# Softmax attention keys kept once for each head of a pair, with zeros on the other head's rows

## The chip, the core and the metric

The kernel runs on one core of one Trainium2 chip. The metric is the device time of one execution in microseconds (us), the median of several runs. The core has five engines that run beside one another and meet through semaphores: TensorE (PE, the matrix engine; its weight loads are listed apart as PEld), VectorE (DVE), ScalarE (ACT), GpSimd (POOL) and SyncE (SP, which issues DMAs). A matmul has a stationary operand, which is loaded first (a weight load), and a moving one that streams against it.

## What is computed

One decoder block on 512 tokens of 1024 features, all float32. Cut to what matters here:

```python
h    = rms_norm(x, norm1_g)
proj = h @ w_in                      # 9744 columns, cut into the parts of all branches
A    = dilated_attention(...)        # softmax attention, 3 groups of 8 heads of 64 features
B    = gated_linear_attention(...)
mixed = sigmoid(gA) * (A @ w_attn_branch) + sigmoid(gB) * (B @ w_gla_branch)
x    = x + mixed @ w_out
x    = x + relu(rms_norm(x) @ w_ff_up) ** 2 @ w_ff_down

# inside a group of the softmax attention, a head with E = 64 features
scores = (q @ k.T) * E ** -0.5       # q, k: rms_norm over the 64 features of the head, with gains
scores = where(valid, scores, -inf)
p      = exp(scores - max(scores))
o      = (p @ v) / sum(p)
```

The three groups look back over windows of 128, 512 and 2048 tokens with dilations 1, 4 and 16. Their outputs are merged by the softmax denominators.

## The kernel before

Weights come in as raw float32 tiles by SP's DMA queue (`raw_load`, line 112), are cut on ACT and DVE into two float32r parts that add up to them (`split`), and go through PE three times: high by high, low by high, high by low. `mm_tok` (lines 151 to 153) makes tokens by features, with the normed input as the stationary operand; `mm_cols` (lines 132 to 134) makes features by tokens, with the weights as the stationary operand. These projections fill most of PE's time. Helper `act` (line 74) records every ACT activation, `tt` (line 77) every DVE tensor-by-tensor operation.

The softmax attention has two parts around the change. `qkv(g, ...)` projects one group: queries, keys, values, one after the other through `mm_tok`. For each of four tiles of 128 tokens it evicts the bank (ACT), squares (POOL), reduces and scales (DVE, ACT), and puts off a `turn`: four transposes on PE (line 324) and one eviction on ACT that writes the transposed tile. These turns are issued while the next projection runs, behind a matmul of it. The transposed queries `q1T`, `q2T`, `q3T` and keys `k1T`, `k2T`, `k3T` have the shape [128, 4, 512]: 128 rows are the 64 features of two heads, 4 is the pair of heads, 512 are tokens. The keys are scaled on the way by the column `gqk`.

`attend` makes one tile of 128 queries for all 8 heads. The score of a head is one f32 matmul whose operands are the 64 rows of that head (`r`, rows 0 to 63 or 64 to 127). It is written into a bank of the pool `aux` (three banks). DVE adds the mask and takes the maximum (line 353), ACT the exponential, PE transposes (line 359), DVE copies the transposed tile to SBUF (line 361), PE multiplies with the values (line 365). `scores1` (line 375) serves the first group with 128 or 256 keys, directly behind `qkv(0)`; `scores23` (line 390) serves the other two groups together, 128 keys each, behind `qkv(1)` and `qkv(2)`. The second and third group use the tokens in permuted order (`hT.perm`, every fourth column).

The order on each engine is made by a scheduler from the program: it fills PE between the steps of `attend` with matmuls of the next projections, so scores, transposes, value matmuls and projections alternate on PE. Big tiles live in 16 numbered slots, `slot(i, ...)`, and a slot is written again only when its readers are done. Slots 14 and 15 were empty until the linear attention's `qT` and `kT`, and slot 10 goes from `k1T` to the linear attention's values.

Of the kernel before, what the change touches and what calls it, by code (L numbers as in the profile page):

```python
# [8 lines left out]
F32 = mybir.dt.float32  # L9
# [3 lines left out]
AF = mybir.ActivationFunctionType  # L13
# [3 lines left out]
P = 128  # L17
S = 512
# [4 lines left out]
E = 64  # L23
# [18 lines left out]
def kernel(ctx: ExitStack, tc: tile.TileContext, x, norm1_g, w_in, q_g, k_g,  # L42
                             gate_up, gate_bias, out_g, branch_bias, w_attn, w_gla, w_out,
                             norm2_g, w_up, w_down, out):
    nc = tc.nc
# [12 lines left out]
    def slot(i, shape, name, dt=F32):  # L58
        return slots.tile(shape, dt, name=name, tag=f"s{i}")
# [13 lines left out]
    def act(o, i, f, **kw):  # L73
        nc.scalar.activation(o, i, f, **kw)  # L74
# [8 lines left out]

# [1 line left out]
    ident = consts.tile([P, P], F32, name="ident")  # L85
# [8 lines left out]

# [1 line left out]
    n_split = [0]  # L96
# [18 lines left out]
    def w_cols(w, nk, c0, n):  # L115
        """weights as the stationary operand: yields (hi, lo) of [P, nk, 128], one output block each"""
        step = 2048 // nk
        piece = 1024 // nk
        for c in range(c0, c0 + n, step):
            raw = raw_load(w, 0, nk, c, step)  # L120
            for q in range(0, step, piece):
                hi, lo = split(raw[:, :, q:q + piece], [nk, piece])
                for b in range(0, piece, P):
                    yield hi[:, :, b:b + P], lo[:, :, b:b + P]

    def mm_cols(wp, rhs, nk):
        """[128 features, 512 tokens] = block^T . rhs"""
        b = mm_bank()
        hi, lo = wp
        for k in range(nk):  # L130
            rh, rl = rhs(k)
            nc.tensor.matmul(b, hi[:, k], rh, start=(k == 0), stop=False)  # L132
            nc.tensor.matmul(b, hi[:, k], rl, start=False, stop=False)  # L133
            mm = nc.tensor.matmul(b, lo[:, k], rh, start=False, stop=(k == nk - 1))  # L134
            if turns and k in (3, 7):
                with tc.issue_after(mm.ins):
                    turns.pop(0)()
        return b

    def mm_tok(w, c0, lhs, r0=0, nk=KB):  # L140
        """four banks [128 tokens, 512 features] = lhs^T . w[:, c0:c0+512]"""
        banks = [mm_bank() for _ in range(NT)]
# [16 lines left out]
    class Split:  # L159
        """[128 features, nk blocks, 512 tokens] in two float32r parts"""  # L160

# [15 lines left out]
    def rsqrt(o, ss, n, w):  # L177
        """o = (ss / n + eps) ** -0.5, with a Newton step behind the tables"""
        v = sm(w, "rv")
        nc.vector.tensor_scalar(v, ss, 1.0 / n, EPS, op0=OP.mult, op1=OP.add)  # L180
        y = sm(w, "ry")
        act(y, v, AF.Ln)
        act(y, y, AF.Exp, scale=-0.5)
        nc.vector.scalar_tensor_tensor(v, y, -0.5, v, op0=OP.mult, op1=OP.mult)
        tt(v, v, y, OP.mult)
        nc.vector.scalar_tensor_tensor(o, v, 1.5, y, op0=OP.add, op1=OP.mult)

# [1 line left out]
    hT = Split("hT", (0, 1), (2, 3))  # L189
# [55 lines left out]

# [1 line left out]
    with tc.issue_after(last.ins):  # L247
        qk_cols = consts.tile([P, 2], F32, name="qk_cols")
        for j, g in enumerate((q_g, k_g)):
            for hf in range(2):  # L250
# [3 lines left out]
                                       op0=OP.mult, op1=OP.mult)  # L254
        # attention masks: 0 where the key is visible, a large negative number elsewhere
        mask_a = consts.tile([P, 256], F32, name="mask_a")
# [14 lines left out]

        # gated linear attention: which (s, t) pairs a level of the block tree covers
        def block_mask(name, w, segs):
            """segs: (offset, groups, columns a group, rows a group, first row, rows); 1 where row s is covered"""
            g = consts.tile([P, w], U8, name=name)
# [25 lines left out]

# [1 line left out]
    def qkv(g, lhs, sq, sk, sv):  # L303
        res = []
        for kind, s in ((0, sq), (1, sk)):
            banks = mm_tok(w_in, kind * 1536 + g * 512, lhs)
            dst = slot(s, [P, 4, S], f"a{kind}{g}")
            for i in range(NT):
# [11 lines left out]

                def turn(s2=s2, d=dst[:, :, i * P:(i + 1) * P], kw={"scale": gqk} if kind else {}):
                    b = aux()
                    for k in range(4):
                        nc.tensor.transpose(b[:, k * P:(k + 1) * P], s2[:, k * P:(k + 1) * P], ident)  # L324
                    act(d, b.rearrange("p (k t) -> p k t", k=4), AF.Copy, **kw)

                later.append(turn)
            res.append(dst)
        banks = mm_tok(w_in, 3072 + g * 512, lhs)
# [9 lines left out]
    def attend(o_idx, i, scores, values, width, mask, dst):  # L339
        """one tile of 128 queries, all 8 heads; scores/values give the parts of `width` keys"""  # L340
        ob = aux()
# [26 lines left out]

    q1T, k1T, v1 = qkv(0, hT.nat, 9, 10, 11)
    o1 = slot(12, [P, NT, 512], "o1")  # L370

    def scores1(dst, pr, hf, i):
        r = slice(hf * E, hf * E + E)
        lo = max(i - 1, 0) * P
        nc.tensor.matmul(dst, q1T[r, pr, i * P:(i + 1) * P], k1T[r, pr, lo:(i + 1) * P], start=True, stop=True)  # L375

# [5 lines left out]

    q2T, k2T, v2 = qkv(1, hT.perm, 4, 5, 6)
    q3T, k3T, v3 = qkv(2, hT.perm, 7, 8, 13)
    o23 = slot(9, [P, NT, 512], "o23")

    def scores23(dst, pr, hf, i):
        r = slice(hf * E, hf * E + E)
        for n, (q_, k_) in enumerate(((q2T, k2T), (q3T, k3T))):
            nc.tensor.matmul(dst[:, n * P:(n + 1) * P], q_[r, pr, i * P:(i + 1) * P],  # L390
                             k_[r, pr, i * P:(i + 1) * P], start=True, stop=True)

    for i in range(NT):
        attend(1, i, scores23, lambda n, s, i: (v2, v3)[n][:, i, s * E:(s + 1) * E], 256, mask_b, o23)

# [1 line left out]
    lse = consts.tile([P, 64], F32, name="lse")  # L397
# [39 lines left out]

# [1 line left out]
    qT = slot(14, [P, GH, S], "qT")  # L439
# [12 lines left out]
    v_proj(1)  # L452
    # the low-rank gate, both factors in two parts each, all four products in one pass over 128 rows
    lowrank = slot(7, [P, 2, S], "lowrank", F32R)
# [18 lines left out]

# [1 line left out]
    cc = slot(6, [P, GH, S], "cc")  # L475
# [17 lines left out]
    for h in range(GH):  # L493
# [5 lines left out]
        def scores2(left, M):  # L499
            """[s, t] products of each tile's 128 tokens with its 192 columns of M, two tiles a bank"""  # L500
            for i2 in range(2):
# [5 lines left out]

        # the diagonal, and blocks of one token
        M = wide("M")
# [5 lines left out]
        for pd, bv in scores2(kh, M):  # L515
            tt(pd, bv[:, :, :P], ident[:, None, :].to_broadcast([P, 2, P]), OP.mult)
            nc.vector.copy_predicated(pd.rearrange("p i (b two) -> p i b two", two=2)[:, :, :, 1],
                                      pair_mask[1][:, :128].rearrange("p (i b) -> p i b", i=2), bv[:, :, P:])
        # groups of four blocks of m tokens, every pair of blocks in a group
        for m in (2, 8):  # L520
# [18 lines left out]
            for pd, bv in scores2(K, M):  # L539
                for a, off in enumerate((0, 96, 160)):  # L540
# [3 lines left out]
                        pd.rearrange("p i (g x) -> p i g x", g=G)[:, :, :, (a + 1) * m:], gx(qmv), gx(bv))  # L544
        # pairs of blocks of 32 and of 64 tokens
        pdiag = pp.rearrange("p i t -> p (i t)")
        for m in (32, 64):
# [17 lines left out]
            else:  # L565
                act(blocks(pdiag, m)[:64, :, 1], bg[:64, :256].rearrange("p (b m) -> p b m", m=m), AF.Copy)
        # tiles below the diagonal
        c3 = ch.rearrange("p (i t) -> p i t", t=P)
# [9 lines left out]
        act(gt, end.rearrange("p i o -> p (i o)"), AF.Exp, scale=1.0 / TAU)  # L578
        # the state before each tile: [channels, values]
        b = aux()  # L580
# [29 lines left out]

# [1 line left out]
    def gate(f, wp, o):  # L612
        b = mm_cols(wp, hT.rhs, KB)
        # sigmoid(z) = exp(min(z, 0) - ln(1 + exp(-|z|))), z = b + bias
        with tc.high_priority():
# [15 lines left out]

# [1 line left out]
    rs = [slot(14 + j, [P, 2, D], f"rs{j}") for j in range(2)]  # L633
# [13 lines left out]

# [1 line left out]
    oT = Split("oT", (6, 8), (4, 5))  # L649
# [15 lines left out]

# [1 line left out]
    gb = [slot(10 + j, [P, 4, S], f"gb{j}") for j in range(2)]  # L667
# [4 lines left out]

# [1 line left out]
    mx = Split("mx", (0, 1), (2, 3))  # L674
# [8 lines left out]

    # ---- output projection, residual; the second norm's scale is left for the end, since
    # relu(r * u) ** 2 = r ** 2 * relu(u) ** 2 for r > 0 ----
    x2 = [slot(s, [P, 2, D], f"x2{s}") for s in (12, 9)]
# [26 lines left out]

# [1 line left out]
    for half in range(2):  # L715
# [48 lines left out]
```

## Time and profile before

| | us |
|---|---|
| device time, median of 3 runs | 1067.73 (1067.21 to 1067.97) |
| span of the profiled execution | 1065.5 |
| PE busy | 1044.1 (98%) |
| weight loads (PEld) busy | 879.0 (82%) |
| DVE busy | 518.3 (49%) |
| ACT busy | 433.5 (41%) |
| POOL busy | 74.2 (7%) |

The profiled execution's own time is its span; the runs without a profile are 2.2 us above it in the median. PE's clock was granted in full in all slices of the page. Matmul ends are modelled, since matmuls are pipelined: a busy PE need not be PE at its peak, and the start of one matmul to the start of the next tells more than the busy share. A timeline row merges neighbours of the same kind: its length runs from the first start to the last end, and xN is how many they are.

### The profile page before, as it was taken

Reading aid. Unit: us, or ns where it says so; the run is one execution under the profiler, and the core shown is the slowest. Engines: PE = TensorE matmul, PEld = TensorE weight load, DVE = VectorE, ACT = ScalarE, POOL = GpSimd, SP = SyncE. Lnnn points to the kernel's source line nnn. Section 1 sums busy time; section 2 is a strip of 40 time slices with the busy share of each in tenths; the row PEclk is TensorE's granted clock in tenths of the full one; section 3 lists DMA queues with packets and bytes.
Section 4 is the critical chain, followed back from the end, with each engine's and each line's share of the span. In section 5 each row is a group of like instructions: output and inputs, shape, how many; then the busy total and the mean of one; then the engine's idle time right before and its main releaser. Section 6 shows DMA issues by size and latency. Waiting matters only on the chain.

```text
span 1065.5 us, 12435 instructions
## 1 busy us (share of the span) xinstructions
PE 1044.1 (98%) x4888; PEld 879.0 (82%) x4888; DVE 518.3 (49%) x928; ACT 433.5 (41%) x763; POOL 74.2 (7%) x112
## 2 busy tenths in 40 slices
PE   4999999999999999999999999999999999999998
PEld 3888889999888788788888888888888888888886
DVE  4644454434444623988856645444442324444231
ACT  4434343424434424766556852333442113433110
POOL 9110001001000000010103000000000000000000
PEclk9999999999999999999999999999999999999999
DMA  7222102322200223221122232442232323232221
GB/s 257 80 80 79 40 3 78 109 89 79 79 28 17 89 80 99 80 79 54 66 67 93 79 106 92 139 138 79 93 104 81 117 80 119 79 117 82 96 102 39
DMA packets 64505, 92.36 MB, mean 87 GB/s; under 512 B 3328, under 2 KB 37120, under 8 KB 64448
## 3 DMA queue, kind: packets, MB, share of 16 engines
q1 hardware_dynamic: 61056, 86.02, 24.8%
q10 hardware_dynamic: 2976, 5.28, 1.4%
q8 instruction: 38, 0.62, 0.2%
q0 software_dynamic: 416, 0.28, 0.2%
q14 instruction: 19, 0.16, 0.0%
HBM read 89.44 MB, written 2.13 MB: 86 GB/s over the span
## 4 chain that ended last, share of the span: by engine, by line
PE 93%; DVE 3%; ACT 2%; DMA 1%; issue 0%; SPq 0%
PE mm L151 16%; PE mm L153 16%; PE mm L152 16%; PE mm L132 11%; PE mm L133 11%; PE mm L134 10%; PE aux L365 2%; PE aux L390 2%; PE aux L359 2%; PE aux L375 1%; DMA raw<-in_w_in_dram 1%; PE aux L504 1%; PE aux L324 1%; PE aux L602 1%; PE aux L559 1%; DVE wlo L77 1%
## 5 line engine op out<-in xcount | busy, mean ns | idle before, releaser
L77 DVE TENSOR_TENSOR wlo<-wraw,whi 128x1024 fp32r<-128x1024 f32 x157 | 192.5, 1226 | 292.5 <-ACT whi L74 290.7
L74 ACT ACTIVATE whi<-wraw 128x1024 fp32r<-128x1024 f32 x157 | 166.1, 1058 | 330.8 <-PE mm L153 224.9
L151 PE MATMUL mm<-whi,hTh 128*128 128x512 f32 x416 | 171.5, 412 | 4.4 <-ACT hTh L74 4.4
L153 PE MATMUL mm<-whi,hTl 128*128 128x512 f32 x416 | 167.4, 403 | 0.0
L152 PE MATMUL mm<-wlo,hTh 128*128 128x512 f32 x416 | 166.4, 400 | 0.0
L151 PEld LDWEIGHTS mm<-whi,hTh 128*128 128x128 f32 x416 | 102.3, 246 | 15.2 <-ACT hTh L74 5.5
L152 PEld LDWEIGHTS mm<-wlo,hTh 128*128 128x128 f32 x416 | 102.4, 246 | 9.9 <-issue 1.0
L153 PEld LDWEIGHTS mm<-whi,hTl 128*128 128x128 f32 x416 | 102.0, 245 | 10.3 <-issue 1.0
L134 PE MATMUL mm<-xgh,wlo 128*128 128x512 f32 x256 | 99.7, 389 | 0.0
L132 PE MATMUL mm<-xgh,whi 128*128 128x512 f32 x256 | 99.7, 389 | 0.0
L133 PE MATMUL mm<-xgl,whi 128*128 128x512 f32 x256 | 99.6, 389 | 0.0
L132 PE MATMUL mm<-hTh,whi 128*128 128x512 f32 x192 | 77.6, 404 | 0.0
L134 PE MATMUL mm<-hTh,wlo 128*128 128x512 f32 x192 | 76.4, 398 | 0.0
L133 PE MATMUL mm<-hTl,whi 128*128 128x512 f32 x192 | 76.4, 398 | 0.0
L133 PEld LDWEIGHTS mm<-xgl,whi 128*128 128x128 f32 x256 | 48.1, 188 | 10.0
L134 PEld LDWEIGHTS mm<-xgh,wlo 128*128 128x128 f32 x256 | 48.0, 188 | 9.9
L132 PEld LDWEIGHTS mm<-xgh,whi 128*128 128x128 f32 x256 | 48.1, 188 | 9.9
L74 ACT ACTIVATE p<-p,nmx 128x256 f32<-128x256 f32 (+1 forms) x64 | 31.2, 488 | 59.9 <-DVE nmx L353 59.9
L361 DVE COPY pt<-aux 128x512 f32<-128x512 f32 (+1 forms) x32 | 21.1, 659 | 65.0 <-PE aux L359 64.7
L151 PE MATMUL mm<-whi,f0h 128*128 128x512 f32 x128 | 49.8, 389 | 0.0
L152 PE MATMUL mm<-wlo,f0h 128*128 128x512 f32 x128 | 49.8, 389 | 0.0
L153 PE MATMUL mm<-whi,f0l 128*128 128x512 f32 x128 | 49.8, 389 | 0.0
(223 smaller groups left out, 1688.5 us busy)
## 6 DMA issues: line engine op xcount, KB each, us to landing
wraw<-in_w_in_dram SPq DMA_DIRECT2D x36, 1024.0 KB, 5.1
wraw<-in_w_ff_up_dram SPq DMA_DIRECT2D x16, 1024.0 KB, 5.4
wraw<-in_w_ff_down_dram SPq DMA_DIRECT2D x16, 1024.0 KB, 5.0
wraw<-in_w_gla_branch_dram SPq DMA_DIRECT2D x4, 1024.0 KB, 5.1
wraw<-in_w_out_dram SPq DMA_DIRECT2D x4, 1024.0 KB, 5.2
raw<-in_w_in_dram SPq DMA_DIRECT2D x2, 1024.0 KB, 14.2
wraw<-in_w_attn_branch_dram SPq DMA_DIRECT2D x2, 1024.0 KB, 5.2
xr<-in_x_dram ACTq DMA_DIRECT2D x8, 256.0 KB, 4.4
```

The costliest lines, as they stand in the source:

```text
L74: nc.scalar.activation(o, i, f, **kw)
L77: return nc.vector.tensor_tensor(o, a, b, op)
L132: nc.tensor.matmul(b, hi[:, k], rh, start=(k == 0), stop=False)
L133: nc.tensor.matmul(b, hi[:, k], rl, start=False, stop=False)
L134: mm = nc.tensor.matmul(b, lo[:, k], rh, start=False, stop=(k == nk - 1))
L151: nc.tensor.matmul(banks[i], lh, hi[:, kk], start=(k == 0), stop=False)
L152: nc.tensor.matmul(banks[i], lh, lo[:, kk], start=False, stop=False)
L153: mm = nc.tensor.matmul(banks[i], ll, hi[:, kk], start=False, stop=(k == nk - 1))
L359: nc.tensor.transpose(tb[:, n * P:(n + 1) * P], p2[:, n * P:(n + 1) * P], ident)
L361: nc.vector.tensor_copy(pt[:, :w2], tb[:, :w2])
L365: nc.tensor.matmul(ob[:, s * E:(s + 1) * E], pt[:, (m * nk + n) * P:(m * nk + n + 1) * P], values(n, s, i), start=(n == 0), stop=(n == nk ...
L390: nc.tensor.matmul(dst[:, n * P:(n + 1) * P], q_[r, pr, i * P:(i + 1) * P], k_[r, pr, i * P:(i + 1) * P], start=True, stop=True)
```

## The change

The transposed keys are kept twice. Each copy has 128 rows, and on it the rows of one of the two heads are zero: the eviction in `turn` runs once for each copy and scales by one of the two columns of the new constant `gqk2`, which holds `gqk` on 64 rows and 0 on the others. A score matmul then uses all 128 rows of the queries and of the copy of its head. The products on the other head's rows are zeros, so the sum is the same. The second copies lie in slots 14 (`k1T`), 15 (`k2T`) and 10 (`k3T`).

```diff
+        gqk2 = consts.tile([P, 2], F32, name="gqk2")
+        nc.vector.memset(gqk2, 0.0)
+        for hf in range(2):
+            nc.vector.tensor_copy(gqk2[hf * E:(hf + 1) * E, hf:hf + 1], gqk[hf * E:(hf + 1) * E])
...
     def qkv(g, lhs, sq, sk, sv):
         res = []
-        for kind, s in ((0, sq), (1, sk)):
+        for kind, ss_ in ((0, sq), (1, sk)):
             banks = mm_tok(w_in, kind * 1536 + g * 512, lhs)
-            dst = slot(s, [P, 4, S], f"a{kind}{g}")
+            dst = [slot(s, [P, 4, S], f"a{kind}{g}{n}") for n, s in enumerate(ss_)]
...
-                def turn(s2=s2, d=dst[:, :, i * P:(i + 1) * P], kw={"scale": gqk} if kind else {}):
+                def turn(s2=s2, dst=dst, i=i, kind=kind):
                     b = aux()
                     for k in range(4):
                         nc.tensor.transpose(b[:, k * P:(k + 1) * P], s2[:, k * P:(k + 1) * P], ident)
-                    act(d, b.rearrange("p (k t) -> p k t", k=4), AF.Copy, **kw)
+                    for n, d in enumerate(dst):
+                        act(d[:, :, i * P:(i + 1) * P], b.rearrange("p (k t) -> p k t", k=4), AF.Copy,
+                            **({"scale": gqk2[:, n:n + 1]} if kind else {}))
...
-            res.append(dst)
+            res.append(dst if kind else dst[0])
...
-    q1T, k1T, v1 = qkv(0, hT.nat, 9, 10, 11)
+    q1T, k1T, v1 = qkv(0, hT.nat, (9,), (10, 14), 11)
...
     def scores1(dst, pr, hf, i):
-        r = slice(hf * E, hf * E + E)
         lo = max(i - 1, 0) * P
-        nc.tensor.matmul(dst, q1T[r, pr, i * P:(i + 1) * P], k1T[r, pr, lo:(i + 1) * P], start=True, stop=True)
+        nc.tensor.matmul(dst, q1T[:, pr, i * P:(i + 1) * P], k1T[hf][:, pr, lo:(i + 1) * P], start=True, stop=True)
...
-    q2T, k2T, v2 = qkv(1, hT.perm, 4, 5, 6)
-    q3T, k3T, v3 = qkv(2, hT.perm, 7, 8, 13)
+    q2T, k2T, v2 = qkv(1, hT.perm, (4,), (5, 15), 6)
+    q3T, k3T, v3 = qkv(2, hT.perm, (7,), (8, 10), 13)
...
     def scores23(dst, pr, hf, i):
-        r = slice(hf * E, hf * E + E)
         for n, (q_, k_) in enumerate(((q2T, k2T), (q3T, k3T))):
-            nc.tensor.matmul(dst[:, n * P:(n + 1) * P], q_[r, pr, i * P:(i + 1) * P],
-                             k_[r, pr, i * P:(i + 1) * P], start=True, stop=True)
+            nc.tensor.matmul(dst[:, n * P:(n + 1) * P], q_[:, pr, i * P:(i + 1) * P],
+                             k_[hf][:, pr, i * P:(i + 1) * P], start=True, stop=True)
```

No matmul is added, and the order of PE's, POOL's and SP's instructions stays as it was. On PE at the first scores of the first attention, with `a10` for `k1T` and `a00` for `q1T`, there stood before:

```order
L152 MATMUL mm_697<-wlo_805,hTh1_84 128x512
L153 MATMUL mm_697<-whi_804,hTl1_86 128x512
L375 MATMUL aux_845<-a10_629,a00_420 128x128
L375 MATMUL aux_846<-a10_629,a00_420 128x128
L375 MATMUL aux_845<-a10_629,a00_420 128x128
L375 MATMUL aux_846<-a10_629,a00_420 128x128
L151 MATMUL mm_1140<-whi_1146,hTh0_83 128x512
L152 MATMUL mm_1140<-wlo_1147,hTh0_83 128x512
```

and now, with `a100` and `a101` for the two copies of the keys:

```order
L152 MATMUL mm_702<-wlo_813,hTh1_84 128x512
L153 MATMUL mm_702<-whi_812,hTl1_86 128x512
L383 MATMUL aux_854<-a100_633,a000_424 128x128
L383 MATMUL aux_855<-a101_634,a000_424 128x128
L383 MATMUL aux_854<-a100_633,a000_424 128x128
L383 MATMUL aux_855<-a101_634,a000_424 128x128
L151 MATMUL mm_1149<-whi_1155,hTh0_83 128x512
L152 MATMUL mm_1149<-wlo_1156,hTh0_83 128x512
```

The same matmuls stand in the same places; the two heads now read two tiles instead of two halves of one. On ACT, while the values of the first group are projected, there stood before:

```order
L74 ACTIVATE ry_655<-rv_653 128x8
L74 ACTIVATE ry_655<-ry_655 128x8
L74 ACTIVATE whi_1146<-wraw_1144 128x1024
L74 ACTIVATE whi_1174<-wraw_1144 128x1024
L74 ACTIVATE a10_629<-aux_756,gqk_233 128x4x128
```

and now:

```order
L74 ACTIVATE ry_660<-rv_658 128x8
L74 ACTIVATE ry_660<-ry_660 128x8
L74 ACTIVATE whi_1155<-wraw_1153 128x1024
L74 ACTIVATE whi_1183<-wraw_1153 128x1024
L74 ACTIVATE a100_633<-aux_761,gqk2_235 128x4x128
L74 ACTIVATE a101_634<-aux_761,gqk2_235 128x4x128
L74 ACTIVATE ry_676<-rv_674 128x8
```

A second eviction of the same bank stands right behind each of the twelve evictions of keys; nothing else on ACT has changed places.

## Rows read from the trace of the kernel before

**Rows 1.** The page: span, and the chain that ended last by engine.
```profile
span 1065.5 us, 12435 instructions
PE 93%; DVE 3%; ACT 2%; DMA 1%; issue 0%; SPq 0%
```

**Rows 2.** Busy time in two stretches, 92.31:157.40 and 278.57:344.30 us, summed.
```profile
sum 130.82, PE 130.79 PEld 106.72 DVE 56.53 ACT 52.99 POOL 2.69; mean PE 65.39 PEld 53.36 DVE 28.27 ACT 26.49 POOL 1.35
```

**Rows 3.** PE's timeline, second attention: start us, length us, line, out<-in, shapes, count.
```profile
285.43 0.38 PE L359 MATMUL aux<-ident,p 128*128 128x128 f32 x2
285.74 0.48 PE L390 MATMUL aux<-a,a 64*128 64x128 f32 x2
286.15 0.44 PE L359 MATMUL aux<-ident,p 128*128 128x128 f32 x2
286.52 0.93 PE L390 MATMUL aux<-a,a 64*128 64x128 f32 x6
287.38 0.50 PE L133 MATMUL mm<-hTl,whi 128*128 128x512 f32 x1
287.72 1.00 PE L365 MATMUL aux<-v,pt 128*128 128x64 f32 x8
```

**Rows 4.** PE's timeline, first attention, 256 keys wide.
```profile
112.88 0.44 PE L359 MATMUL aux<-ident,p 128*128 128x128 f32 x2
113.25 0.70 PE L375 MATMUL aux<-a,a 64*128 64x256 f32 x2
113.87 0.62 PE L153 MATMUL mm<-whi,hTl 128*128 128x512 f32 x1
114.33 0.40 PE L151 MATMUL mm<-whi,hTh 128*128 128x512 f32 x1
```

**Rows 5.** PE's timeline around the block of sixteen score records.
```profile
278.25 0.40 PE L153 MATMUL mm<-whi,hTl 128*128 128x512 f32 x1
278.57 1.26 PE L390 MATMUL aux<-a,a 64*128 64x128 f32 x16
279.76 0.50 PE L132 MATMUL mm<-hTh,whi 128*128 128x512 f32 x1
280.10 0.40 PE L133 MATMUL mm<-hTl,whi 128*128 128x512 f32 x1
280.33 0.40 PE L134 MATMUL mm<-hTh,wlo 128*128 128x512 f32 x1
```

**Rows 6.** PE's timeline: the first block of scores, what follows, the last block.
```profile
92.31 0.72 PE L375 MATMUL aux<-a,a 64*128 64x128 f32 x8
92.96 0.62 PE L151 MATMUL mm<-whi,hTh 128*128 128x512 f32 x1
...
337.53 1.16 PE L390 MATMUL aux<-a,a 64*128 64x128 f32 x8
```

**Rows 7.** PE's timeline in the linear attention: f32 matmuls over 128 rows.
```profile
468.59 0.59 PE L602 MATMUL aux<-vg,pps 128*128 128x256 f32 x2
469.02 0.59 PE L604 MATMUL aux<-st,q 128*128 128x256 f32 x2
```

**Rows 8.** Lines 359 and 375: durations in ns, least/median/most, first and last start.
```profile
L359 PE MATMUL aux<-ident,p x120: 270/272/332, 94.4 to 342.3; 128*128 128x128 f32 x120
L375 PE MATMUL aux<-a,a x64: 272/376/480, 92.3 to 150.8; 64*128 64x256 f32 x48, 64*128 64x128 f32 x16
```

**Rows 9.** Weight loads' timeline: one of contiguous columns, two of every fourth column.
```profile
287.38 0.19 PEld L133 LDWEIGHTS mm<-hTl,whi 128*128 128x128 f32 x1
...
113.87 0.31 PEld L153 LDWEIGHTS mm<-whi,hTl 128*128 128x128 f32 x1 [0.33 <-issue]
114.08 0.33 PEld L151 LDWEIGHTS mm<-whi,hTh 128*128 128x128 f32 x1
```

**Rows 10.** DVE's timeline: the copy that the value matmuls at 287.72 read.
```profile
286.63 0.69 DVE L361 COPY pt<-aux 128x512 f32<-128x512 f32 x1 [2.27 <-PE aux L359]
```

**Rows 11.** ACT's timeline ahead of the first attention's exponentials.
```profile
89.65 0.69 ACT L74 ACTIVATE a<-aux,gqk 128x512 f32<-128x512 f32 x1 [1.21 <-PE aux L324]
90.35 2.67 ACT L74 ACTIVATE v<-mm 128x512 f32<-128x512 f32 x4
92.91 1.05 ACT L74 ACTIVATE whi<-wraw 128x1024 fp32r<-128x1024 f32 x1
93.86 0.39 ACT L74 ACTIVATE p<-p,nmx 128x128 f32<-128x128 f32 x1
```

## The prediction

> **What bounds the kernel now.** Read the page first: the span is 1065.5 us and TensorE (PE) has 93% of the chain that ended last [rows 1]. A change on another engine therefore counts only where PE comes to wait for it. Then cut out the two stretches in which the softmax scores are computed, 92.31 to 157.40 us and 278.57 to 344.30 us: PE is busy for 130.79 of 130.82 us, VectorE (DVE) for 56.53 and ScalarE (ACT) for 52.99 [rows 2]. But "busy" does not mean that the time is well used. The ends of matmuls are modelled, so what counts is the distance from one start to the next. Look at how the starts stand around the score matmuls (line 375 for the first attention, line 390 for the second). Each f32 product of the program is two records, so there are 64 and 128. They stand on PE in 43 unbroken blocks, the first at 92.31 us and the last at 337.53 us [rows 6].
>
> A run of n records is as long as its starts lie apart plus one duration, 0.27 us for transposes and for 128-wide scores, 0.38 us for 256-wide ones [rows 8]. Two undisturbed transposes take 0.38 us, so their starts are 0.38 - 0.27 = 0.11 us apart. In the block of six scores at 286.52 us the reader sees four losses [rows 3]:
> - **Entry.** The second transpose before it starts at 286.15 + 0.44 - 0.27 = 286.32; the first score follows 0.20 us later, not 0.11: 0.09 lost.
> - **Second record.** The two scores at 285.74 last 0.48 in all, so the second starts 0.48 - 0.27 = 0.21 behind the first. In the six, the other four starts are (0.93 - 0.27 - 0.21) / 4 = 0.112 apart: 0.10 lost.
> - **Exit.** The last score starts at 286.52 + 0.93 - 0.27 = 287.18, the projection behind it at 287.38, 0.20 later: 0.09 lost.
> - **Behind the exit.** That projection needs 0.34 us to the next start, where the undisturbed distance is 280.33 - 280.10 = 0.23 [rows 5]: 0.11 lost. Where transposes come next, their second start is 0.44 - 0.27 = 0.17 away, not 0.11: 0.06 lost.
>
> The 256-wide blocks of the first attention show the same [rows 4]: entry 0.20; the second start 0.70 - 0.38 = 0.32 away; exit 113.87 - 113.57 = 0.30. Full-height f32 matmuls of the same width (lines 602 and 604, 128 rows) run at (469.02 - 468.59) / 2 = 0.215 us with no gap at all, even between two lines [rows 7]. So 0.10 and 0.09 are lost here too. When the next work is a projection whose weights are every fourth column, its next start is 0.46 away: 0.23 lost. Such a weight load lasts 0.31 us, the contiguous one 0.19, and the next follows it 0.21 later [rows 9].
>
> **The change part by part.** *Scores over 128 rows.* All score operands now have 128 rows, as everything around them. Nothing gets wider or more frequent: 192 records before and after. I take a score record at the interior distance that both heights show: 0.112 us at 128 columns, 0.215 at 256. I take the four losses as gone, because the only difference between the runs that have them and the runs that don't is the number of rows.
> - 25 blocks with transposes behind: 25 x (0.09 + 0.10 + 0.09 + 0.06) = 8.5 us.
> - 8 blocks with a contiguous projection behind: 8 x (0.09 + 0.10 + 0.09 + 0.11) = 3.1 us.
> - 8 blocks with a strided projection behind: 8 x (0.28 + 0.23) = 4.1 us if the 0.21 us load fits behind a 0.215 us score; 2.2 us if none of the 0.23 goes.
>
> The two blocks left over are unlike the rest: the two heads alternate, and their 64-row matmuls overlap in pairs. 16 records take 279.76 - 278.57 = 1.19 us [rows 5]; at full height 16 x 0.112 = 1.79, a loss of 0.60. Its entry (0.32 instead of 0.23) and the projection behind it (0.34) give back 0.20: net -0.4. The 8 records at 92.31 take 0.65 us [rows 6] and become 0.90; entry and exit give back about as much: 0. Gross gain 8.5 + 3.1 + 4.1 - 0.4 = 15.3 us.
>
> A rule speaks against the change here. The rows say that 24 of the 192 records ran in pairs. The Trainium skill, TensorEngine Tiling (Array Packing), "When to Use Tiling", says that a contraction of 64 should use two row tiles, which work in parallel, for up to twice the speed. As an estimate by it, 144 x 0.112 + 48 x 0.215 = 26.4 us of scores could have been 13.2, and the change would cost up to 13.2 us; the trace disagrees for the other 41 blocks, which gain nothing from it today.
>
> *New waits.* The value matmuls at 287.72 need a DVE copy that ends at 286.63 + 0.69 = 287.32 [rows 10, 3]: 0.40 us to spare. Between the transposes that feed the copy and these matmuls the losses that go are 0.09 + 0.10 + 0.09 + 0.11 = 0.39, so the spare time is just used up. I take 0.05 us of new wait for such a place and 16 places (two a tile of queries, 8 tiles): 0.8 us; bounds 0 and 16 x 0.2 = 3.2. The masks and exponentials sit on engines that are 43% and 41% busy [rows 2] and move with the scores.
>
> *Twelve more evictions on ACT* (the second copy of the keys), 0.69 us each [rows 11], 8.3 us in all. PE reaches them only through what stands behind them on ACT: evictions of V, a weight split, the first exponentials. The first three of each four come earlier, while projections run and PE waits for nothing of ACT. The fourth stands right ahead of the V evictions, at 89.65 us, and from there to the exponentials at 93.86 ACT has no idle time [rows 11]; up to 0.7 us can reach the transposes there. Three groups: 0 to 2.0 us; I take 0.5, since in the second group no attention follows and in the third the longer block of 16 hides it. A memset and two copies of one column on DVE, at set-up, lie beside matmuls: nothing. No DMA is added, and SP's and POOL's queues keep their order. The slots that the copies use are rewritten only behind the last scores that read them.
>
> **Sum.** 15.3 - 0.8 - 0.5 = 14.0 us. The profiled span of 1065.5 becomes 1051.5. The median of the runs, 1067.73, lies 2.2 above that span; I carry this over: 1053.7 us. Behind 344 us nothing changes, and since PE is the chain there the gain should reach the end.
>
> **The rivals.**
> - *The chain through DVE and ACT takes over.* The gaps go, but PE waits for copies and exponentials instead, and half the gain is lost: 1060.7. For it: the spare time of 0.40 above. Against it: DVE and ACT are idle for more than half of both stretches.
> - *The gaps stay.* They would belong to the switch between transposes and f32 products, or to a wait, not to the rows. Then only the pairs (0.60 + 0.25) and ACT's 0.5 are lost: 1069.1, no change. Against it: entry and exit have the same size whatever stands beside the block [rows 3, 4], and lines 602 and 604 change over without one [rows 7].
> - *Slower: weight loads of full height are no longer hidden.* The second record of each block shows what a score costs whose load is not hidden: 0.21 and 0.32. If that held for every score, the 86 further records in the 41 blocks would pay 86 x 0.10 = 8.6, the paired 24 would go from 0.65 + 1.19 to 24 x 0.21 = 5.0, another 3.2, and the gaps would stay: 1079.5. It decides at a spacing of 0.21 instead of 0.11 inside blocks. Against it: [rows 7], full height, two different stationary operands in turn, 0.215 at 256 columns.
>
> The Trainium skill, TensorE: Matmul & The Clock Gate, "Part 3: Packing small matmuls", says that a weight load overlaps running matmuls only where its group of rows differs. By that rule the slower rival is what happens; the full-height runs of this trace disagree.
>
> **How the numbers follow.** Forecast 0.80, chain takes over 0.09, gaps stay 0.05, loads exposed 0.06. The forecast's own bounds: 15.3 with no give-back and somewhat more at the two paired blocks gives 1052; without the strided share (1.9), with 3.2 of waits and 2.0 on ACT, 8.2 is left, 1059.5. All of these at once is unlikely, so the range is 1051.5 to 1058.5. About 0.2% (2.1 us) is what a measurement of this kernel can tell from no change: faster 0.89, same 0.05, slower 0.06.
>
> **What would show it.** In the changed trace: scores as 128*128 with starts 0.11 and 0.215 apart from the first record on; about 0.11 between a transpose and a score, both ways; the block of 16 at 1.8 us; the first stretch some 7 us shorter and the second some 7; new waits of value matmuls for the copies under 0.1 us each; equal distances behind the second attention. I am wrong if the second record still comes 0.21 or 0.32 behind the first, if gaps of 0.2 remain at the edges, or if PE's starts move apart at the value matmuls or at the first transposes of an attention.

## The result and the profile after

The changed kernel takes 1054.25 us in the median (1053.82 to 1054.79) against 1067.85 (1067.21 to 1068.75) of the kernel before beside it: a ratio of 0.9875, with a 95% interval from 0.9861 to 0.9889. That is 13.6 us less; forecast were 14.0 less, a time of 1053.7 and a range from 1051.5 to 1058.5. The span of the profiled execution went from 1065.5 to 1052.1 us. Lines 359, 365, 375 and 390 of before are lines 368, 374, 383 and 397 of after.

The page of after, where [rows 1] stood for before: span, busy time with the share and the instructions of PE and ACT, and the chain by engine.

```profile
span 1052.1 us, 12454 instructions
PE 1030.6 (98%) x4888; PEld 877.8 (83%) x4888; DVE 517.4 (49%) x931; ACT 439.4 (42%) x775; POOL 74.9 (7%) x112
...
PE 93%; DVE 3%; DMA 2%; ACT 2%; issue 0%; SPq 0%; DVEq 0%; ACTq 0%
```

PE makes the same 4888 matmuls in 13.5 us less busy time and is as busy as before. The busy share told nothing of the loss, and tells nothing of its end.

The two attentions from their first score to their last group of value matmuls, in the windows view: before, then after. The columns are the stretch, its length, and the busy time and count of each engine.

```profile
92.31:157.11 64.80, 64.80 (x328) 53.49 (x327) 28.49 (x92) 26.27 (x81) 2.08 (x2) 1.00 0.10 33
278.57:343.37 64.80, 64.77 (x408) 52.02 (x408) 27.83 (x85) 25.71 (x77) 0.61 (x1) 1.00 0.11 34
```

```profile
91.76:149.67 57.91, 57.91 (x327) 53.73 (x326) 28.18 (x92) 26.31 (x81) 2.08 (x2) 1.00 0.11 37
270.98:329.84 58.86, 58.86 (x408) 50.85 (x407) 27.34 (x85) 25.74 (x77) 1.58 (x1) 1.00 0.12 37
```

The same matmuls take 6.9 us less in the first stretch and 5.9 less in the second, whose stretch of after begins 0.03 ahead of the score at 271.01 (forecast: some 7 each). That is 12.8 of the 13.4 us by which the spans differ. Another 0.5 is won ahead of the first score, most of it in the opening transposes. That half microsecond is not the change's: a second profile of the changed kernel, taken for "The new waits" below, has its first score at 92.38 us, no earlier than before. Behind the second attention the traces agree to 0.2 us.

PE's timeline of after in the second attention, the place of [rows 3], and in the first, the place of [rows 4]:

```profile
278.07 0.38 PE L368 MATMUL aux<-ident,p 128*128 128x128 f32 x2
278.28 0.39 PE L397 MATMUL aux<-a,a 128*128 128x128 f32 x2
278.51 0.38 PE L368 MATMUL aux<-ident,p 128*128 128x128 f32 x2
278.73 0.83 PE L397 MATMUL aux<-a,a 128*128 128x128 f32 x6
279.31 0.48 PE L133 MATMUL mm<-hTl,whi 128*128 128x512 f32 x1
279.67 1.10 PE L374 MATMUL aux<-v,pt 128*128 128x64 f32 x8
...
110.55 0.60 PE L383 MATMUL aux<-a,a 128*128 128x256 f32 x2
```

From the first transposes to the value matmuls this stretch took 287.72 - 285.43 = 2.29 us before and takes 279.67 - 278.07 = 1.60 now, 0.69 less for two blocks. The four losses are gone. Two scores take 0.39 in all, so their starts are 0.39 - 0.27 = 0.12 apart, where it was 0.21. The second pair of transposes has the undisturbed length of 0.38, where it was 0.44. The entry at 278.28 lies 278.28 - (278.07 + 0.38 - 0.27) = 0.10 behind the last transpose, where it was 0.20. The 256-wide pair takes 0.60 where it took 0.70. The projection behind the six scores starts 279.31 - (278.73 + 0.83 - 0.27) = 0.02 behind the last of them, where it was 0.20.

Only the split at the exit is not the prediction's. It took 0.09 for the exit and 0.11 for the projection behind it. Measured are 0.18 for the exit here; and the next start behind such a projection stays 0.31 us away (273.03 - 272.72, in the rows of "The pairs" below), where it was 0.34. The sum of the two, 0.20, is as taken.

One thing is worse. The value matmuls at 279.67 take 1.10 us where those at 287.72 took 1.00. The sources view of that line tells why, before (line 365) and after (line 374); each says how long, and how often, the weight loads (PEld) of these matmuls stood idle until the DVE copy was done:

```profile
its engine sat idle before it (us, times) until:
  DVE pt L361: 2.6, 9
```

```profile
its engine sat idle before it (us, times) until:
  DVE pt L370: 5.0, 21
```

The view counts twelve waits more than before. The copied tile `pt` is the stationary operand of the value matmuls, so its first reader is a weight load. The copy in front of 279.67 is this row of DVE; it ends at 279.62, and the load follows it at once:

```profile
278.93 0.69 DVE L370 COPY pt<-aux 128x512 f32<-128x512 f32 x1 [1.92 <-PE aux L368]
279.67 0.41 PEld L374 LDWEIGHTS aux<-v,pt 128*128 128x128 f32 x3 [0.19 <-DVE pt L370]
```

Before, the load in front of the matmuls at 287.72 was this one, 287.49 - 287.32 = 0.17 us behind the copy of [rows 10]:

```profile
287.49 1.09 PEld L365 LDWEIGHTS aux<-v,pt 128*128 128x128 f32 x8
```

Over all 32 groups of value matmuls, the first load starts 0.05 us behind the end of its copy in 18 groups before, and in all 32 now. In the other 14 it had started 0.17 to 0.31 us behind it.

### The profile page after: what moved, and what is told of

Read it like the earlier page. It is cut to its first block, busy times and chain, and to the rows that moved or that the text cites. A ratio compares the mean times of both kernels' runs of the same rounds, so it can differ in the third digit from the quotient of the medians.

```text
span 1052.1 us, 12454 instructions
## 1 busy us (share of the span) xinstructions
PE 1030.6 (98%) x4888; PEld 877.8 (83%) x4888; DVE 517.4 (49%) x931; ACT 439.4 (42%) x775; POOL 74.9 (7%) x112
## 4 chain that ended last, share of the span: by engine, by line
PE 93%; DVE 3%; DMA 2%; ACT 2%; issue 0%; SPq 0%; DVEq 0%; ACTq 0%
PE mm L151 16%; PE mm L153 16%; PE mm L152 16%; PE mm L132 11%; PE mm L133 11%; PE mm L134 11%; PE aux L374 3%; PE aux L397 1%; PE aux L368 1%; DMA raw<-in_w_in_dram 1%; PE aux L383 1%; PE aux L511 1%; PE aux L331 1%; PE aux L609 1%; PE aux L566 1%; ACT whi L74 1%
## 5 line engine op out<-in xcount | busy, mean ns | idle before, releaser
L151 PE MATMUL mm<-whi,f1h 128*128 128x512 f32 x128 | 49.8, 389 | 0.0
L152 PE MATMUL mm<-wlo,f1h 128*128 128x512 f32 x128 | 49.8, 389 | 0.0
## 6 DMA issues: line engine op xcount, KB each, us to landing
raw<-in_w_in_dram SPq DMA_DIRECT2D x2, 1024.0 KB, 14.1
```

Source lines behind the costliest of these rows:

```text
L151: nc.tensor.matmul(banks[i], lh, hi[:, kk], start=(k == 0), stop=False)
L152: nc.tensor.matmul(banks[i], lh, lo[:, kk], start=False, stop=False)
```

## The experiments

The theory: the gain lies at the edges where PE goes from 128-row work to 64-row work and back. Rivals: it comes from the new slots and the new order on ACT; the gaps belong to the place of the scores (a wait for a bank, for DVE, for ACT); the rest of the gain is held up by a chain through DVE and ACT. Each job ran its own executions of the kernel before on its chip (medians 1067.00, 1067.29 and 1067.22 us), so ratios are compared, and differences are taken inside a job.

**Two copies, 64 rows.** The second copy of the keys is written, and no score uses its height:

```diff
-        nc.tensor.matmul(dst, q1T[:, pr, i * P:(i + 1) * P], k1T[hf][:, pr, lo:(i + 1) * P], start=True, stop=True)
+        r = slice(hf * E, hf * E + E)
+        nc.tensor.matmul(dst, q1T[r, pr, i * P:(i + 1) * P], k1T[hf][r, pr, lo:(i + 1) * P], start=True, stop=True)
```

and the same in `scores23`.

> The changed kernel with one thing undone: both copies of the keys are written, but each score matmul reads only the 64 rows of its head. Edges theory (the gain lies at the edges between 64-row and 128-row work on PE): the gaps are back, and what is left is the price of twelve evictions: 1067.9 to 1068.9 us. Rival (the gain came from the other slots and the changed order of evictions): 1054 to 1056 us.

Measured: 1066.95 us against 1067.00, ratio 0.9999 (0.9990 to 1.0009). The gain is gone and the gaps are back, so neither slots nor the order on ACT made it. The price of the evictions is not there either: it is within 1 us of nothing (the expected 1067.9 to 1068.9 was written beside a kernel before of 1067.85, so it meant 0 to 1 us). In the traces, this kernel and the one before differ by less than 0.1 us inside the two attentions. PE's timeline of this kernel, at the place of [rows 3]:

```profile
285.17 0.38 PE L368 MATMUL aux<-ident,p 128*128 128x128 f32 x2
285.48 0.49 PE L399 MATMUL aux<-a,a 64*128 64x128 f32 x2
285.90 0.44 PE L368 MATMUL aux<-ident,p 128*128 128x128 f32 x2
286.26 0.93 PE L399 MATMUL aux<-a,a 64*128 64x128 f32 x6
```

These are the distances of before, to 0.01 us.

**128 rows, one copy.** The kernel before with all rows in every score (`r = slice(0, P)` twice); the zeros on the other head's rows are left out, and each score holds two heads' sum.

> The kernel before with scores over all 128 rows of one copy of the keys; the zeros on the other head's rows are left out, so each score holds the sum of two heads. Edges theory: the whole gain without the twelve evictions, 1053.3 to 1054.3 us, that is 0 to 1 us under the changed kernel. If the evictions cost nothing, 1054.2. Rival (the copies matter, not the rows): 1066 to 1068 us.

Measured: 1053.77 us against 1067.00, ratio 0.9876 (0.9861 to 0.9891), the same as the changed kernel's 0.9875. The rows alone make the gain. Twelve evictions more or less can't be told apart.

**Each attention alone.** `scores1` with 128 rows and `scores23` with 64, and the other way round.

> 128 rows in the first attention alone, 64 in the second. Edges theory, from the start-to-start sums over the 21 blocks of the two traces (7.8 us less, a little lost to waits): 1060.0 to 1060.9 us.

> 128 rows in the second attention alone, 64 in the first. Edges theory, from the sums over its 22 blocks (6.6 us less): 1061.2 to 1062.2 us; together with the other half the gains add up to that of the whole change. If a chain through DVE and ACT limited the gain, the two halves would add up to more than the whole.

Measured: 1059.89 us for the first (ratio 0.9933, 0.9917 to 0.9950) and 1060.87 for the second (0.9941, 0.9926 to 0.9956), against 1067.00. That is 7.1 and 6.1 us, together 13.2; the kernel with 128 rows in both gained 13.2 in the same job. Both came out 0.1 to 0.3 us under their range, since the kernel before was 0.85 us faster on this chip than on the first one. The halves add up, so no chain that spans both attentions limits the gain.

**A lone product, with nothing to wait for.** Into the feed-forward projections of the changed kernel go 64 f32 products of constants, each behind twelve projection matmuls; N is 128 or 64 rows, and a third kernel takes 64 columns of the stationary operand.

```diff
+    def probe():
+        nc.tensor.matmul(aux()[:, :P], ident[:N], ident[:N], start=True, stop=True)
...
+        turns.extend([probe] * 32)
         for f, wp in enumerate(w_cols(w_up, KB, half * 2048, 2048)):
```

> The changed kernel with 64 added f32 products of 128 rows and 128 columns in the feed-forward projections, one behind every twelfth matmul, each into a bank that nobody reads and with operands that wait for nothing. Edges theory: only their own two records of 0.112 us each, 64 x 0.22 to 0.23 = 14.1 to 14.8 us over the changed kernel: 1068.4 to 1069.1 us.

> The same 64 added products, with 64 rows instead of 128. Edges theory: two records and the four losses of a lone block in front of a contiguous projection, 64 x (0.22 + 0.39) = 39 us: 1093.0 to 1094.5 us. Rival (the gaps belong to the place of the scores: a wait for a bank, for DVE or ACT): the same as with 128 rows, 1068.4 to 1069.1 us.

> The same 64 added products, 128 rows high, but with a stationary operand of 64 columns. If every change of the array's shape has the edges, about as with 64 rows: 1092 to 1094.5 us. If they belong to the rows alone: 1067 to 1069 us.

Measured, against 1067.29 of the kernel before: 1071.93 us with 128 rows (ratio 1.0044, 1.0029 to 1.0059), 1095.44 with 64 rows (1.0263, 1.0247 to 1.0278), 1092.04 with 64 columns (1.0230, 1.0213 to 1.0247). Half the rows cost 23.5 us more than all of them, 23.5 / 64 = 0.37 us for each product, where 0.39 was expected. Nothing but the shape differs, and the order on all engines is the same. PE's timeline around one product, 128 rows, then 64 rows, then 64 columns:

```profile
714.23 0.40 PE L134 MATMUL mm<-xgh,wlo 128*128 128x512 f32 x1
714.46 0.38 PE L723 MATMUL aux<-ident 128*128 128x128 f32 x2
714.60 0.48 PE L132 MATMUL mm<-xgh,whi 128*128 128x512 f32 x1
714.91 0.40 PE L133 MATMUL mm<-xgl,whi 128*128 128x512 f32 x1
```

```profile
712.95 0.39 PE L134 MATMUL mm<-xgh,wlo 128*128 128x512 f32 x1
713.27 0.49 PE L723 MATMUL aux<-ident 64*128 64x128 f32 x2
713.69 0.50 PE L132 MATMUL mm<-xgh,whi 128*128 128x512 f32 x1
714.02 0.39 PE L133 MATMUL mm<-xgl,whi 128*128 128x512 f32 x1
```

```profile
716.17 0.39 PE L134 MATMUL mm<-xgh,wlo 128*128 128x512 f32 x1
716.49 0.43 PE L723 MATMUL aux<-ident 128*64 128x128 f32 x2
716.85 0.50 PE L132 MATMUL mm<-xgh,whi 128*128 128x512 f32 x1
717.19 0.39 PE L133 MATMUL mm<-xgl,whi 128*128 128x512 f32 x1
```

From the projection ahead to the second one behind it is 0.68 us at full height, 1.07 with 64 rows, 1.02 with 64 columns. Entry (0.32 instead of 0.23), exit (0.20 instead of 0.03) and the projection behind (0.33 or 0.34 instead of 0.31) are alike in both cut shapes; the second record starts 0.21 behind the first with 64 rows, 0.16 with 64 columns and 0.11 at full size. It is the change of shape that costs, in rows as in columns, and not the place. The level at full height was missed by some 3 us: the kernel takes 18.0 us more than the changed one would in this job (0.9875 x 1067.29 = 1053.95), instead of 14.1 to 14.8. The 64-row kernel lies 0.9 us over its range, and the 64-column kernel just inside its own. Behind a product of full height the projections run a little wider for some 10 steps, 0.05 us in all, which makes up the 3 us. Why they do, no run tells.

**The pairs.** The first block of the second attention reads 64 rows again; all others read 128:

```diff
+            r = slice(hf * E, hf * E + E) if i == 0 and pr < 2 else slice(0, P)
-            nc.tensor.matmul(dst[:, n * P:(n + 1) * P], q_[:, pr, i * P:(i + 1) * P],
-                             k_[hf][:, pr, i * P:(i + 1) * P], start=True, stop=True)
+            nc.tensor.matmul(dst[:, n * P:(n + 1) * P], q_[r, pr, i * P:(i + 1) * P],
+                             k_[hf][r, pr, i * P:(i + 1) * P], start=True, stop=True)
```

> The changed kernel, but the first block of the second attention (16 records, in which the two heads alternate) reads 64 rows as before. Pairs theory: that block takes 0.4 us less, 1053.9 us, visible in the trace rather than in the time. If the loss of overlap costs nothing: 1054.2 us.

Measured: 1053.96 us, ratio 0.9875 (0.9860 to 0.9890), no difference that the runs can tell. PE's timeline of the block in the changed kernel and in this one, with the first transposes behind it:

```profile
270.79 0.39 PE L153 MATMUL mm<-whi,hTl 128*128 128x512 f32 x1
271.01 1.95 PE L397 MATMUL aux<-a,a 128*128 128x128 f32 x16
272.72 0.48 PE L132 MATMUL mm<-hTh,whi 128*128 128x512 f32 x1
273.03 0.40 PE L133 MATMUL mm<-hTl,whi 128*128 128x512 f32 x1
...
273.49 0.39 PE L132 MATMUL mm<-hTh,whi 128*128 128x512 f32 x1
273.72 0.39 PE L368 MATMUL aux<-ident,p 128*128 128x128 f32 x2
```

```profile
271.56 0.40 PE L153 MATMUL mm<-whi,hTl 128*128 128x512 f32 x1
271.89 1.26 PE L398 MATMUL aux<-a,a 64*128 64x128 f32 x16
273.08 0.50 PE L132 MATMUL mm<-hTh,whi 128*128 128x512 f32 x1
273.42 0.39 PE L133 MATMUL mm<-hTl,whi 128*128 128x512 f32 x1
...
273.88 0.40 PE L132 MATMUL mm<-hTh,whi 128*128 128x512 f32 x1
274.21 0.44 PE L368 MATMUL aux<-ident,p 128*128 128x128 f32 x2
```

From the projection ahead to the second one behind, 2.24 us became 1.86: the pairs save 0.38, as expected. But the transposes that follow now come 0.33 behind their predecessor instead of 0.23, and the next ones lose as much again: they wait for exponentials. What the block wins goes for the most part into those waits.

**The new waits.** If the value matmuls wait for the DVE copy, a copy in two halves should let the first of them go sooner:

```diff
-                nc.vector.tensor_copy(pt[:, :w2], tb[:, :w2])
+                for m in range(2):
+                    nc.vector.tensor_copy(pt[:, m * width:(m + 1) * width], tb[:, m * width:(m + 1) * width])
```

> The changed kernel unchanged, beside the next two on the same chip: ratio 0.987 to 0.988 to the kernel before.

> The changed kernel with the DVE copy of the transposed tile made in two halves, so that the first value matmuls wait for half of it. Theory (14 to 16 value blocks now wait 0.10 to 0.14 us each for that copy): PE gains 1 to 2 us, 1052.3 to 1053.3 us where the changed kernel takes 1054.3. Rival (they wait for nothing, the wider spacing of their first records is PE's own): the same time, or slower by the longer queue on DVE, 32 x 0.15 us of work. The scheduler places some projections of the first attention in another order.

> Both edits together, copies in halves and 64 rows for the first block of the second attention: another 0.4 us less than the copies in halves alone, 1051.9 to 1052.9 us.

Measured, against 1067.22: the changed kernel 1054.11 us (ratio 0.9876, 0.9861 to 0.9891), copies in halves 1054.31 (0.9879, 0.9863 to 0.9896), both edits 1053.91 (0.9874, 0.9860 to 0.9889). All three are the same. In the sources view the value matmuls' idle time until the copy fell from 5.0 us in 21 places to this:

```profile
  DVE pt L371: 3.2, 13
```

So the waits are waits for the copy, and fewer, but PE gained nothing. The value matmuls now stand in 60 groups instead of 32, and the scheduler had placed other projections between them; which of the two took the 1 to 2 us back is not shown. This part of the expectation failed, and no version beats the changed kernel by more than the runs can tell.

## Why the prediction was right, step by step

- **The four losses are one cause, and they go.** Summed from the start ahead of each of the 43 blocks to the second start behind it, the two timelines give 53.96 us before and 39.57 after, 14.4 us less, where 15.3 were taken; one distance that lies between two neighbouring blocks is in both, and counted once it is 14.2. By the prediction's kinds: 25 blocks with transposes behind 8.1 (8.5 taken), 8 with a contiguous projection 2.8 (3.1), 8 with a strided one 4.0 (4.1), the two paired blocks -0.4 (-0.4). The kernel with two copies and 64 rows, the one with 128 rows and one copy, and the lone product show that it is the shape.
- **The term that was too large**, by the most, is the lone block behind value matmuls: 0.29 instead of 0.34 in each of eleven blocks that have transposes behind. The second score behind a value matmul still starts 0.17 us after the first (280.79 after 280.62 in this row's 0.44 - 0.27), not 0.11. The row is cut after two of the block's eight records, where the window of the view ends:

```profile
280.62 0.44 PE L397 MATMUL aux<-a,a 128*128 128x128 f32 x2
```

- **The strided load is hidden** behind a 256-wide score, as taken: six of the eight blocks gain about 0.50 or more and the other two 0.45 and 0.46. The lower bound of 2.2 for this term was too careful.
- **New waits** stand at the place that was named, and are larger: the value matmuls spread by 1.10 - 1.00 = 0.10 us at 14 places, not 0.05 at 16. The prediction had misread the spare time. It counted 0.40 us from the end of the copy to the first matmul, but the reader that came first was the weight load, 0.17 behind the copy, and a load that waits starts 0.05 behind it: 0.12 to spare, where 0.39 went. In 18 groups there was none at all. Away from the blocks the two timelines lose 1.2 us inside the attentions: 1.5 in new waits, less 0.3 at the first transposes of the second attention, which waited for exponentials before and wait less behind the longer block of 16.
- **The evictions cost nothing** that was measured, instead of 0.5: without them 0.9876, with them 0.9875. ACT's timeline shows where they went. Count from the first score of each trace (92.31 before, 91.76 now). The V evictions started 92.31 - 90.35 = 1.96 us ahead of it [rows 11] and now start 91.76 - 90.37 = 1.39 ahead, 0.57 later. But they follow each other almost without waits and take 2.19 us, not 2.67, so that the exponentials start 93.40 - 91.76 = 1.64 behind the first score, where it was 1.55. The prediction took ACT to have no idle time there; the merged row of [rows 11] hid some, 2.67 - 4 x 0.60 = 0.27 us between four evictions of 0.60 each.

```profile
90.37 2.19 ACT L74 ACTIVATE v<-mm 128x512 f32<-128x512 f32 x4
...
93.40 0.39 ACT L74 ACTIVATE p<-p,nmx 128x128 f32<-128x128 f32 x1
```

- **The sum** is 1 us more than the change makes, and part of its closeness is luck. Of 15.3 at the blocks 14.2 came (counted once), and the 0.8 + 0.5 = 1.3 that was taken off for waits and ACT was 1.2, all of it waits: 14.2 - 1.2 = 13.0, where 14.0 were forecast. The spans differ by 13.4 because the execution profiled of the changed kernel was 0.4 us quicker ahead of the attentions; the medians differ by 13.6 within an interval of 1.5 us either way. The second profile of the changed kernel has the same 14.2 and 1.2, and its span of 1052.5 is 13.0 under that of before. The later jobs, each beside its own kernel before, give 13.1 for the changed kernel and 13.2 for the one with 128 rows and one copy.
- **The rivals.** The gaps did not stay, and the weight loads of full height stay hidden: scores are 0.11 and 0.22 us apart. Half-height products ran side by side only in the two blocks in which the two heads alternate, and the longer one lost 0.38 us by the change; the rule of two row tiles bore on nothing else here, which is why the change pays where blocks hold one head at a time.

## To carry to other kernels

Measure matmuls from start to start, not by busy time: a PE that was busy for 98% lost 0.3 to 0.6 us at every short run of half-height products between full-height work. Where such runs are short and not interleaved between the halves, padding the contraction with zeros to the full 128 rows is cheaper, as long as the copy that makes the zeros lies on an engine with spare time. Whether it would pay more to let the heads alternate in every block was not run. When PE then gets faster, look at who hands it its next operand with the least time to spare, counted to the weight load where that operand is the stationary one: the loss comes back there first.

## What the runs showed of the hardware that was not expected

- A stationary operand of 64 columns pays nearly the same edges as one of 64 rows: 1.02 and 1.07 us from start to start over a lone product, 0.68 at full size. In time that is (1092.04 - 1071.93) / 64 = 0.31 and 0.37 us a product.
- After one f32 product of full size the next ten or so float32r projections run a little wider, 0.05 us in all (0.02 after one of 64 rows): 64 products cost 18.0 us, 0.28 each, where the stretch up to the second start behind accounts for 0.68 - 2 x 0.227 = 0.23.
